# Prefix log-sum-exp on one core: three time steps per partition in place of two, Exp written over x, and later rows added to PSUM by VectorE

## The chip, the cores and the metric

The kernel runs on one NeuronCore of one Trainium2 chip. The metric is device time in microseconds (us), the median of several executions. Beside them stands one profiled execution, whose trace holds every instruction and every DMA packet with start and duration.

## What is computed

The input `x` has shape (4, 4096, 4128) in fp32: a batch of 4, 4096 time steps, 4128 features. The output is the running log-sum-exp along time:

```
out[:, 0, :] = x[:, 0, :]
for t in range(1, S):
    mx = max(out[:, t-1, :], x[:, t, :])
    out[:, t, :] = mx + log(exp(out[:, t-1, :] - mx) + exp(x[:, t, :] - mx))
```

That equals `log(cumsum(exp(x)))` along time, and so both kernels compute it: exponentials in fp16, a prefix sum by matmul in fp32 in PSUM, a logarithm, and a carry from tile to tile.

## The kernel before

One *tile* is a block of 256 consecutive time steps (`rows = P * R`, 128 partitions by `R = 2` rows, line 61) with all 4128 features. Partition p holds time steps 2p and 2p+1, one run of 33,024 bytes in device memory. There are 64 tiles, 16 for each batch, and each is loaded once and stored once (4128 KB each way).

The features of a tile are cut into four chunks of 1024 columns (`CH`); the last 32 columns, the *tail*, go with the fourth chunk. `Step.run` (lines 155 to 173) writes the order of all work out by hand under a manual schedule, so each engine takes its instructions in the order of the calls:

- `exp(c)` (line 107): ScalarE computes Exp of both rows of a chunk in one instruction, 128 x 2048 elements, into a separate fp16 tile `et` (pool of 4).
- `head(c)` (line 114): TensorE builds the prefix sum of row 0 in a PSUM tile `pt` of 128 x 1024 fp32 (two banks, pool of 3). Weights `incl` (partitions up to and with p) go with row 0, `excl` (partitions before p) with row 1, and `pick` fetches the carry of the tile before. That is six matmuls of 512 columns, four in the first tile of a batch.
- `ln(j, c)` (line 125): ScalarE writes Ln of the PSUM tile over row j of `xt`, in fp32.
- `second(c)` (line 128): TensorE adds row 1 to the same PSUM tile with two matmuls whose weights are the identity `ident`. `pt` then holds the prefix sum of row 1.
- `close(c)` (line 133): Ln of row 1, then `keep` (line 88): VectorE copies the last 32 partitions of `pt` to fp16 (line 90) and the rounding error beside it (line 91). This is the carry.
- `tail_mm` and `ln_tail` (lines 138, 148) do the same for the tail in a PSUM tile `qt`.

Loads and stores are all issued from SyncE's queue (SP). Five `xt` buffers exist (line 72). The load of tile i+3 is issued ahead of the work and the store of tile i (lines 176 to 184); it waits until the store of tile i-2 has landed, because both use one buffer.

Of the kernel before, what the change touches and what calls it, by code (L numbers as in the profile page):

```python
# [7 lines left out]
FP32 = mybir.dt.float32  # L8
FP16 = mybir.dt.float16
ACT = mybir.ActivationFunctionType  # L10
P = 128
R = 2
CH = 1024
MM = 512
HI, LO = 96, 32


def _constants(nc, pool):


    def tri(base, name):
        t = pool.tile([P, P], FP16, name=name)
        nc.gpsimd.memset(t, 1.0)

        nc.gpsimd.affine_select(  # L25
            out=t, in_=t, pattern=[[1, P]], compare_op=mybir.AluOpType.is_ge,
            fill=0.0, base=base, channel_multiplier=-1,
        )
        return t

    def ones_where_zero(bases, step, name):
        t = pool.tile([P, P], FP16, name=name)
        nc.gpsimd.memset(t, 0.0)
        for base in bases:
            nc.gpsimd.affine_select(  # L35
                out=t, in_=t, pattern=[[step, P]], compare_op=mybir.AluOpType.not_equal,
                fill=1.0, base=base, channel_multiplier=1,
            )
        return t

    return (
        tri(0, "incl"),
        tri(-1, "excl"),
        ones_where_zero([0], -1, "ident"),
        ones_where_zero([-(HI + 31), -(LO + 31)], 0, "pick"),
    )


@with_exitstack
def kernel(  # L50
    ctx: ExitStack,
    tc: tile.TileContext,
    x: bass.AP,
    out: bass.AP,
):

    nc = tc.nc
    B, S, D = x.shape  # L60
    rows = P * R
    n_t = S // rows
    assert S % rows == 0
    n_main = D // CH
    tail = D - n_main * CH
    t0 = n_main * CH

    nc.scalar.preload_act_table_set("natural_log_exp_and_others")  # L68
    consts = ctx.enter_context(tc.tile_pool(name="consts", bufs=1))
    incl, excl, ident, pick = _constants(nc, consts)  # L70

    xpool = ctx.enter_context(tc.tile_pool(name="xpool", bufs=5))
    epool = ctx.enter_context(tc.tile_pool(name="epool", bufs=4))
    cpool = ctx.enter_context(tc.tile_pool(name="cpool", bufs=1))
    pmain = ctx.enter_context(tc.tile_pool(name="pmain", bufs=3, space=bass.MemoryType.PSUM))
    ptail = ctx.enter_context(tc.tile_pool(name="ptail", bufs=2, space=bass.MemoryType.PSUM))

    carry = [cpool.tile([P, CH], FP16, name=f"carry{c}") for c in range(n_main)]
    carry_t = cpool.tile([P, tail], FP16, name="carry_t")
    for t in (*carry, carry_t):  # L80
        nc.vector.memset(t, 0.0)  # L81

    ctx.enter_context(tc.manual_schedule())

    def mm(pt, w, rhs, start, stop):
        nc.tensor.matmul(pt, lhsT=w, rhs=rhs, start=start, stop=stop, skip_group_check=True)  # L86

    def keep(cr, pt):

        nc.vector.tensor_copy(cr[HI:HI + 32, :], pt[HI:HI + 32])  # L90
        nc.vector.tensor_tensor(  # L91
            out=cr[LO:LO + 32, :], in0=pt[HI:HI + 32], in1=cr[HI:HI + 32, :],
            op=mybir.AluOpType.subtract,
        )

    class Step:
        def __init__(self, b, k):
            self.first = k == 0
            self.xt = xpool.tile([P, R, D], FP32, name="xt")
            self.et, self.pt = {}, {}  # L100
            self.dram = lambda t: t[b, k * rows:(k + 1) * rows, :].rearrange("(p j) d -> p j d", j=R)
            nc.sync.dma_start(out=self.xt, in_=self.dram(x))  # L102

        def cols(self, c):
            return slice(c * CH, (c + 1) * CH if c + 1 < n_main else D)

        def exp(self, c):
            s = self.cols(c)
            w = s.stop - s.start
            et = epool.tile([P, R, CH + tail], FP16, name="et")  # L110
            nc.scalar.activation(et[:, :, :w], self.xt[:, :, s], ACT.Exp)  # L111
            self.et[c] = et

        def head(self, c):
            et = self.et[c]
            pt = self.pt[c] = pmain.tile([P, CH], FP32, name="pt")
            for s in range(0, CH, MM):
                mm(pt[:, s:s + MM], incl, et[:, 0, s:s + MM], True, False)
            for s in range(0, CH, MM):
                mm(pt[:, s:s + MM], excl, et[:, 1, s:s + MM], False, self.first)  # L120
            if not self.first:
                for s in range(0, CH, MM):
                    mm(pt[:, s:s + MM], pick, carry[c][:, s:s + MM], False, True)

        def ln(self, j, c):
            nc.scalar.activation(self.xt[:, j, c * CH:(c + 1) * CH], self.pt[c], ACT.Ln)  # L126

        def second(self, c):
            pt = self.pt[c]
            for s in range(0, CH, MM):  # L130
                mm(pt[:, s:s + MM], ident, self.et[c][:, 1, s:s + MM], False, True)

        def close(self, c):

            self.ln(1, c)
            keep(carry[c], self.pt[c])

        def tail_mm(self):
            et = self.et[n_main - 1]
            qt = self.qt = ptail.tile([P, R, tail], FP32, name="qt")  # L140
            e0, e1 = et[:, 0, CH:], et[:, 1, CH:]
            for j in range(R):
                mm(qt[:, j, :], incl, e0, j == 0, False)
                mm(qt[:, j, :], incl if j else excl, e1, False, self.first)
                if not self.first:
                    mm(qt[:, j, :], pick, carry_t, False, True)

        def ln_tail(self):
            nc.scalar.activation(self.xt[:, :, t0:D], self.qt, ACT.Ln)  # L149
            keep(carry_t, self.qt[:, 1, :])  # L150

        def store(self):
            nc.sync.dma_start(out=self.dram(out), in_=self.xt)  # L153

        def run(self):
            last = n_main - 1
            self.exp(0)
            self.head(0)
            for c in range(1, n_main):
                self.exp(c)  # L160
                self.head(c)
                if c == last:
                    self.tail_mm()
                self.ln(0, c - 1)
                self.second(c - 1)
                if c >= 2:
                    self.close(c - 2)
            self.ln(0, last)
            self.second(last)
            self.close(last - 1)  # L170
            self.ln_tail()
            self.close(last)
            self.store()

    work = [(b, k) for b in range(B) for k in range(n_t)]
    ahead = 3
    steps = []
    for i, (b, k) in enumerate(work):
        if i == 0:
            steps += [Step(*work[n]) for n in range(ahead)]  # L180
        if i + ahead < len(work):
            n = i + ahead
            steps.append(Step(*work[n]))
        steps[i].run()


# [28 lines left out]
```

The softmax here doesn't subtract the row's maximum and nothing guards it: scores larger than these inputs give would overflow.

## Time and profile before

| | us |
|---|---|
| median of 10 runs (lowest, highest) | 1265.36 (1264.41, 1266.25) |
| the profiled execution, its own time | 1264.41 |
| its span, first to last instruction | 1262.6 |
| DMA queue of loads and stores, share of 16 engines' span | 99.5% |
| ScalarE busy | 962.6 (76%) |
| TensorE matmul busy | 665.4 (53%) |
| VectorE busy | 655.6 (52%) |

The span is what the instructions of the trace cover; the execution's own time is 1.8 us longer. 541.07 MB pass through the data queue, half in and half out, at a mean of 429 GB/s over the span. Busy shares are means over the span; they do not say which engine is waited for.

### The profile page before, as it was taken

The numbers are of one execution on the slowest core, as the hardware profiler recorded it, in microseconds if no ns is written. First come the engines' busy times: TensorE is split into PE (matmuls) and PEld (weight loads), VectorE is DVE, ScalarE is ACT, GpSimd is POOL, SyncE is SP. The second block draws the span as 40 slices with busy tenths as digits, with TensorE's granted clock in tenths as the row PEclk, the third lists the DMA queues.
The fourth block names the chain that finished last, engine by engine and source line by source line (L and its number), as shares of the span: only waits on it lengthen the run. The fifth ranks groups of instructions, "written<-read, shape, count | busy, mean of one in ns | idle before, by whom it ended". The sixth has DMA issues, their size and how long they took to land.

```text
span 1262.6 us, 7025 instructions
## 1 busy us (share of the span) xinstructions
PE 665.4 (53%) x2392; PEld 242.6 (19%) x2392; DVE 655.6 (52%) x645; ACT 962.6 (76%) x833; POOL 2.2 (0%) x13
## 2 busy tenths in 40 slices
PE   2566655545555465464554645546545555455551
PEld 1222221211112121121111212112112121121210
DVE  3556565464554544545545455464564544645543
ACT  6888887778777777786877878778778787787872
POOL 0000000000000000000000000000000000000000
PEclk9877788778687677867768777777767687777776
DMA  9999999999999999999999999999999999999997
GB/s 402 419 433 432 431 434 427 434 435 425 432 434 434 435 432 432 432 431 431 434 433 435 432 434 433 433 428 434 433 435 432 433 433 431 431 434 433 433 434 336
DMA packets 18466, 541.51 MB, mean 429 GB/s; under 512 B 2048, under 2 KB 2048, under 8 KB 2048
## 3 DMA queue, kind: packets, MB, share of 16 engines
q1 hardware_dynamic: 18432, 541.07, 99.5%
q8 instruction: 19, 0.31, 0.1%
q14 instruction: 15, 0.12, 0.0%
HBM read 270.53 MB, written 270.53 MB: 429 GB/s over the span
## 4 chain that ended last, share of the span: by engine, by line
DMA 84%; ACT 2%; SPq 1%; DVE 1%; issue 1%; PE 0%; ACTq 0%
DMA out_dram<-xt 80%; DMA xt<-in_x_dram 5%; ACT et L111 1%; ACT xt L126 1%; SPq L102 1%; PE pt L86 0%; DVE carry L90 0%; DVE carry L91 0%; SPq L153 0%; DVE carry_t L90 0%; DVE carry_t L91 0%; ACTq L126 0%
## 5 line engine op out<-in xcount | busy, mean ns | idle before, releaser
L90 DVE CAST carry<-pt 32x1024 f16<-32x1024 f32 x256 | 314.8, 1230 | 574.6 <-ACT xt L126 571.7
L126 ACT ACTIVATE xt<-pt 128x1024 f32<-128x1024 f32 x512 | 504.2, 1028 | 127.8 <-PE pt L86 67.1
L111 ACT ACTIVATE et<-xt 128x2048 f16<-128x2048 f32 (+1 forms) x256 | 485.5, 1921 | 148.8 <-DMA xt<-in_x_dram 148.8
L86 PE MATMUL pt<-et,incl 128*128 128x512 f16 x512 | 211.9, 507 | 547.6 <-ACT et L111 373.3
L91 DVE TENSOR_TENSOR carry<-pt,carry 32x1024 f16<-32x1024 f32 x256 | 313.9, 1226 | 8.8
L86 PE MATMUL pt<-et,excl 128*128 128x512 f16 x512 | 211.2, 505 | 0.0
L86 PEld LDWEIGHTS <-incl 128*128 128x128 f16 x704 | 69.2, 111 | 683.1 <-issue 635.5
L86 PE MATMUL pt<-carry,pick 128*128 128x512 f16 x480 | 195.1, 498 | 0.0
L86 PE MATMUL pt<-et,ident 128*128 128x512 f16 x512 | 175.5, 429 | 25.9 <-ACT xt L126 25.9
L86 PEld LDWEIGHTS <-excl 128*128 128x128 f16 x576 | 71.4, 124 | 117.4 <-issue 86.3
L86 PEld LDWEIGHTS <-pick 128*128 128x128 f16 x600 | 69.5, 118 | 94.5 <-issue 65.8
L86 PEld LDWEIGHTS <-ident 128*128 128x128 f16 x512 | 49.5, 106 | 100.5 <-issue 73.7
L86 PE MATMUL qt<-et,incl 128*128 128x32 f16 x192 | 19.9, 191 | 0.0
L86 PE MATMUL qt<-carry_t,pick 128*128 128x32 f16 x120 | 15.6, 182 | 0.0
L149 ACT ACTIVATE xt<-qt 128x64 f32<-128x64 f32 x64 | 14.6, 228 | 0.0
L90 DVE CAST carry_t<-qt 32x32 f16<-32x32 f32 x64 | 12.6, 196 | 2.0
L91 DVE TENSOR_TENSOR carry_t<-qt,carry_t 32x32 f16<-32x32 f32 x64 | 12.4, 193 | 2.2
L86 PE MATMUL qt<-et,excl 128*128 128x32 f16 x64 | 11.7, 183 | 0.0
L81 DVE MEMSET carry<- 128x512 uint32 x4 | 1.9, 485 | 1.1 <-PEq L199 1.0
L68 ACT ACT_TABLE_LOAD x1 | 1.3, 1283 | 0.8 <-PEq L199 0.8
L35 POOL TENSOR_SCALAR_AFFINE_SELECT pick<-pick 128x128 f16<-128x128 f16 x2 | 0.6, 292 | 0.1
L25 POOL TENSOR_SCALAR_AFFINE_SELECT incl<-incl 128x128 f16<-128x128 f16 x1 | 0.3, 292 | 0.0
(11 smaller groups left out, 1.9 us busy)
## 6 DMA issues: line engine op xcount, KB each, us to landing
xt<-in_x_dram SPq DMA_DIRECT2D x64, 4128.0 KB, 29.3
out_dram<-xt SPq DMA_DIRECT2D x64, 4128.0 KB, 38.6
```

Of the source, the lines that this page charges most:

```text
L25: nc.gpsimd.affine_select(out=t, in_=t, pattern=[[1, P]], compare_op=mybir.AluOpType.is_ge, fill=0.0, base=base, channel_multiplier=-1,)
L35: nc.gpsimd.affine_select(out=t, in_=t, pattern=[[step, P]], compare_op=mybir.AluOpType.not_equal, fill=1.0, base=base, channel_multiplier=1,)
L68: nc.scalar.preload_act_table_set("natural_log_exp_and_others")
L81: nc.vector.memset(t, 0.0)
L86: nc.tensor.matmul(pt, lhsT=w, rhs=rhs, start=start, stop=stop, skip_group_check=True)
L90: nc.vector.tensor_copy(cr[HI:HI + 32, :], pt[HI:HI + 32])
L91: nc.vector.tensor_tensor(out=cr[LO:LO + 32, :], in0=pt[HI:HI + 32], in1=cr[HI:HI + 32, :], op=mybir.AluOpType.subtract,)
L102: nc.sync.dma_start(out=self.xt, in_=self.dram(x))
L111: nc.scalar.activation(et[:, :, :w], self.xt[:, :, s], ACT.Exp)
L126: nc.scalar.activation(self.xt[:, j, c * CH:(c + 1) * CH], self.pt[c], ACT.Ln)
L149: nc.scalar.activation(self.xt[:, :, t0:D], self.qt, ACT.Ln)
```

## The change

`R` becomes 3. A tile holds 384 time steps, one run of 49,536 bytes for each partition. A batch has 32 blocks of 128 steps, so it is cut into ten tiles of three rows and one of two; in the first batch the small tile comes first, in the others last. That makes 40 tiles of three rows and 4 of two.

Exp of all three rows of a chunk is one instruction, and its fp16 result is written over the front half of the same fp32 columns of `xt` (`half` is `xt` seen as fp16). The pool `et` is gone, and `xt` has four buffers. The load of tile n+3 is issued after the store of tile n, on the same queue.

`second` and the weights `ident` are gone. After Ln of row j, VectorE adds row j+1 of the exponentials to the PSUM tile in place (`stage`, 128 x 1024, fp32 + fp16). `head` has two matmuls for each row and two for the carry, eight in a tile of three rows. The tail's rows are formed by matmuls with a broadcast right side.

Each tile runs a small pipeline over g: at each g, stage d of chunk g-d for d from high to low, then Exp of chunk g+2 and the head of chunk g+1. Exp of chunks 0 and 1 of the next tile comes after the last stage of this one. The diff, without the constants and the asserts:

```diff
-R = 2
+R = 3
...
-    def mm(pt, w, rhs, start, stop):
-        nc.tensor.matmul(pt, lhsT=w, rhs=rhs, start=start, stop=stop, skip_group_check=True)
+    def mm(pt, w, rhs, start=False):
+        nc.tensor.matmul(pt, lhsT=w, rhs=rhs, start=start, stop=False, skip_group_check=True)
...
-    xpool = ctx.enter_context(tc.tile_pool(name="xpool", bufs=5))
-    epool = ctx.enter_context(tc.tile_pool(name="epool", bufs=4))
+    bufs = 4
+    xpool = ctx.enter_context(tc.tile_pool(name="xpool", bufs=bufs))
...
+        def load(self):
+            full = xpool.tile([P, R, D], FP32, name="xt")
+            self.xt = full[:, :self.r, :]
+            self.half = self.xt.bitcast(FP16)
             nc.sync.dma_start(out=self.xt, in_=self.dram(x))
...
-        def second(self, c):
-            pt = self.pt[c]
-            for s in range(0, CH, MM):
-                mm(pt[:, s:s + MM], ident, self.et[c][:, 1, s:s + MM], False, True)
...
+        def e(self, j, a, b):
+            return self.t.half[:, j, 2 * self.c * CH + a:2 * self.c * CH + b]
+
+        def exp(self):
+            c0, w = self.c * CH, self.w
+            nc.scalar.activation(
+                self.t.half[:, :, 2 * c0:2 * c0 + w], self.t.xt[:, :, c0:c0 + w], ACT.Exp,
+            )
+
+        def head(self):
+            t = self.t
+            pt = self.pt = pmain.tile([P, CH], FP32, name="pt")
+            for j in range(t.r):
+                for s in range(0, CH, MM):
+                    mm(pt[:, s:s + MM], excl if j else incl, self.e(j, s, s + MM), start=j == 0)
+            if not t.first:
+                for s in range(0, CH, MM):
+                    mm(pt[:, s:s + MM], pick, carry[self.c][:, s:s + MM])
+            if self.c == last:
+                self.tail_head()
+
+        def tail_head(self):
+            t, r = self.t, self.t.r
+            full = ptail.tile([P, R, tail], FP32, name="qt")
+            qt = self.qt = full[:, :r, :]
+            to = lambda v, n: v.unsqueeze(1).to_broadcast([P, n, tail])
+            for i in range(r):
+                e = self.e(i, CH, CH + tail)
+                mm(qt[:, i:, :], incl, to(e, r - i), start=i == 0)
+                if i:
+                    mm(qt[:, :i, :], excl, to(e, i))
+            if not t.first:
+                mm(qt, pick, to(carry_t, r))
+
+        def stage(self, j):
+            t, c, pt = self.t, self.c, self.pt
+            nc.scalar.activation(t.xt[:, j, c * CH:(c + 1) * CH], pt, ACT.Ln)
+            if j + 1 < t.r:
+                nc.vector.tensor_tensor(
+                    out=pt, in0=pt, in1=self.e(j + 1, 0, CH), op=mybir.AluOpType.add,
+                )
+                if c == last and j == 0:
+                    nc.scalar.activation(t.xt[:, :, t0:D], self.qt, ACT.Ln)
+                    keep(carry_t, self.qt[:, t.r - 1, :])
+            else:
+                keep(carry[c], pt)
...
+    ahead = bufs - 1
+    for s in steps[:ahead]:
+        s.load()
+    for n, s in enumerate(steps):
+        chunks = [Chunk(s, c) for c in range(n_main)]
+        chunks[0].exp()
+        chunks[1].exp()
+        chunks[0].head()
+        for g in range(n_main + s.r - 1):
+            for d in range(s.r - 1, -1, -1):
+                if 0 <= g - d < n_main:
+                    chunks[g - d].stage(d)
+            if g + 2 < n_main:
+                chunks[g + 2].exp()
+            if g + 1 < n_main:
+                chunks[g + 1].head()
+        s.store()
+        if n + ahead < len(steps):
+            steps[n + ahead].load()
```

## Prediction

> **What bounds the kernel now.** I read the totals and the DMA rows first, then the list of waits, the groups, and last the timeline of one tile.
>
> ```profile
> PE 665.4 (53%) x2392; PEld 242.6 (19%) x2392; DVE 655.6 (52%) x645; ACT 962.6 (76%) x833; POOL 2.2 (0%) x13
> ...
> DMA  9999999999999999999999999999999999999997
> ...
> q1 hardware_dynamic: 18432, 541.07, 99.5%
> ```
> ```profile
> SPq L102 <- DMA out_dram<-xt: 1079.6, 59, 20.4
> ```
> ```profile
> DVE carry L90 <- ACT xt L126: 571.7, 161, 18.7
> ...
> ACT et L111 <- DMA xt<-in_x_dram: 148.8, 55, 11.1
> ```
>
> The data queue is busy for 99.5% of the span in every slice, the loads wait for stores (1079.6 us), ScalarE waits for loads (148.8 us). So the transfers set the end. In the trace a 33,024-byte packet follows another on its engine every 1.219 us, so 16 engines move 433.5 GB/s, and one tile (8.45 MB in and out) takes 19.5 us. The compute of a tile takes, in the last one, from the start of Exp of chunk 0 (1222.40) to the end of the last Ln (1239.95) 17.5 us. The margin is 2 us a tile, and it is what the change spends.
>
> The durations that I use:
>
> ```profile
> L90 DVE CAST carry<-pt 32x1024 f16<-32x1024 f32 x256 | 314.8, 1230 | 574.6 <-ACT xt L126 571.7
> L126 ACT ACTIVATE xt<-pt 128x1024 f32<-128x1024 f32 x512 | 504.2, 1028 | 127.8 <-PE pt L86 67.1
> ...
> L91 DVE TENSOR_TENSOR carry<-pt,carry 32x1024 f16<-32x1024 f32 x256 | 313.9, 1226 | 8.8
> ...
> L86 PE MATMUL pt<-et,ident 128*128 128x512 f16 x512 | 175.5, 429 | 25.9 <-ACT xt L126 25.9
> ```
> ```profile
> L111 ACT ACTIVATE et<-xt 128x2048 f16<-128x2048 f32 x192 | 359.2, 1904 | 148.8 <-DMA xt<-in_x_dram 148.8
> ```
> ```profile
> 1222.40 3.71 ACT L111 ACTIVATE et<-xt 128x2048 f16<-128x2048 f32 x2 [1.80 <-DMA xt<-in_x_dram]
> ...
> 1224.36 1.01 PE L86 MATMUL pt<-et,incl 128*128 128x512 f16 x2 [5.07 <-ACT et L111]
> 1225.17 1.06 PE L86 MATMUL pt<-et,excl 128*128 128x512 f16 x2
> 1226.03 1.06 PE L86 MATMUL pt<-carry,pick 128*128 128x512 f16 x2
> ...
> 1227.17 1.02 ACT L126 ACTIVATE xt<-pt 128x1024 f32<-128x1024 f32 x1 [1.06 <-issue]
> ...
> 1238.95 1.23 DVE L90 CAST carry<-pt 32x1024 f16<-32x1024 f32 x1 [0.94 <-ACT xt L126]
> 1240.22 1.23 DVE L91 TENSOR_TENSOR carry<-pt,carry 32x1024 f16<-32x1024 f32 x1
> 1241.47 0.20 DVE L90 CAST carry_t<-qt 32x32 f16<-32x32 f32 x1
> ```
>
> In the timeline a head of six matmuls takes 2.86 us from the end of the first Exp (1224.31) to Ln (1227.17), pairs following each other by 0.85 us. Two `keep` instructions take 2.52 us (1238.95 to 1241.47).
>
> **What the Trainium skill says.** "VectorE: DVE Perf Modes", section "The perf-mode tier table": tensor_tensor with a PSUM operand runs at one element a cycle. The page's (N+151)/0.96 gives 1.224 us for 1024; line 91 agrees (1.226). "ScalarE: Activation LUTs", section "What ACT_TABLE_LOAD costs": back-to-back ACTIVATEs overlap by about 93 ns; agrees (two Exps, 2 x 1.904 - 3.71 = 0.10). "TensorE: Matmul & The Clock Gate", Part 1: after an idle window of 3.4 us the array runs at half rate, 427 ns for 512 columns. The trace agrees: in 54 places the matmuls start after over 3.4 us without one, and of the first eight at least 87% follow at 0.427.
>
> **The change part by part.** *Transfers.* The bytes are the same. A three-row tile is 12.68 MB both ways, 29.25 us at 433.5 GB/s. Packets for each engine fall from 1024 to 704. At 27.2 B/ns (the 435 GB/s ceiling of "DMA: Bandwidth & Descriptors", Specifications; 433.5 here) a packet would take 1.214 us, so about 5 ns are fixed: 320 x 5 ns = 1.6 us gained at most. Runs of 193.5 x 256 B could give half of that back. *Queue.* On SP a load is now behind the store of tile n, which waits for the tile's last Ln. The load has two more tiles of compute before it is needed, 64 us against some 32 us for a store and a load: no cost; if that cover went, the start of a tile would wait for the load. Four buffers for five: covered likewise. *Exp in place:* same elements, no more work. *Identity matmuls gone:* 175.5 us of TensorE, beside other work; nothing on the path. *VectorE adds:* 40 x 8 + 4 x 4 = 336 of them, a new link between two Lns of the same chunk. No row shows 128 x 1024 from PSUM to PSUM. From below 1.07 us (1024 elements at the page's 0.96 GHz, nothing fixed), from above 1.39 (line 91's 0.16 us over that, counted once more for a write to PSUM); a conflict of read and write is rival B. A gain from the add itself is excluded: it only lengthens the way from Ln to Ln. I take line 91, 1.226, and 1.26 with the start of the next.
>
> *The chain of one three-row tile*, c chunk, r row. In the built order Exp of the next tile comes behind the last Ln of this, and the tail's Ln waits for the add of chunk 3 ahead of it; whatever stands behind it on ScalarE waits too.
>
> 1. Exp c0: 1.904 + (1.904 - 1.028) = 2.78.
> 2. Head of eight cold matmuls until Ln: 2.86 + 2 x 0.427 = 3.71. Exp c1 (2.78) lies beneath.
> 3. ScalarE until Ln of c0 r2 has ended: Ln c0 r0 (0.92 to the next), Exp c2 (2.81), Ln c0 r1 and c1 r0 (1.84), Exp c3 (2.89), Ln (1.02): 9.48.
> 4. VectorE without a gap: keep c0, two adds, keep c1, two adds: 2 x 2.52 + 4 x 1.26 = 10.05. Its Lns are done sooner. The head of c3, which needs the PSUM buffer of c0, is beneath.
> 5. Tail Ln (0.14 to the next), Ln c2 r2 (1.02): 1.16.
> 6. keep c2, then the last add: 2.52 + 1.23 = 3.75.
> 7. Ln c3 r2, until the next Exp: 0.92.
>
> With five handovers of 0.03 (ScalarE to VectorE in the trace): 32.0 us. That is over the 29.25 of the transfers, so the bound moves to the ScalarE-VectorE chain. DMA will wait 9% of the time.
>
> A two-row tile: 1.90 + 2.86 + 0.92 + 1.93 + 1.02, then three times (keep 2.52 + add 1.23 + two handovers 0.06), two Lns between (2.04) and 1.07 at the end = 23.2. The first of a batch has no `pick`: 0.85 less.
>
> Sum: first load landed 13.2 (Exp starts at 13.16 now, same size); first tile 22.3; 37 x 32.0 = 1184; 3 x 31.15 = 93.5; two small tiles 46.4; the last 23.3; its store 12.3 (the first load, issue at 0.80 to landing at 13.1); end 0.3. Together 1395 us of span. The execution's own time was 1.8 over its span, and the median 0.95 over that: 1398.
>
> **The rivals.** *A, the transfers stay the bound: not slower.* The point is a tile chain under 29.25 us. Five adds lie on the chain, so an add of at most 1.226 - 2.75/5 = 0.68 us decides, that is two elements a cycle. For it: fp16 on one input. Against: line 91 has the same kinds of inputs and takes 1.226. Time: 1265.4 - 1.6 + up to 0.8, about 1264. Chance 0.05. *B, the add reads and writes one PSUM bank at half rate:* 2.29 us, 1.07 more, 5 x 40 + 3 x 4 times: +227, 1625. For it: no such row in the trace. Against: nothing there shows a read slowed by other PSUM work. 0.07. *C, the head is not on the path,* because TensorE stays at full rate: Ln then starts when Exp c1 has ended, 0.93 sooner in 43 tiles: 1358. Against: between the head of c3 and the next tile TensorE has some 12 us without work. 0.06. *D, 49.5 KB runs transfer over 9% slower,* with DMA at 99%: 1400 or more; nothing in the profile speaks for it. 0.03.
>
> **How the numbers follow.** The main case has 0.79. Its own range: an add of 1.07 takes 0.156 x 212 = 33 us off, 1365; one of 1.39 adds 35; handovers from VectorE to ScalarE, not shown, of 0.15 as VectorE to TensorE takes (1234.89 to 1235.04 in the trace) in place of 0.03 add two times 0.12 in 44 tiles, 11; both at once would be 1444, which I think improbable, and I stop at 1435. The range 1358 to 1435 takes in C and leaves out A and B. Faster by over 0.2% 0.03, within 0.2% 0.02 (a difference that small couldn't be told from none in this kernel), slower 0.95.
>
> **What would show it.** The data queue's share falls to about 91%; SP's waits for a store to land give way to waits for ScalarE; VectorE busy near 860; Exp starts 32 us apart in three-row tiles; ScalarE has waits for VectorE, absent now, and for TensorE at the tile's start; the new add near 1.23 us. Wrong: a 99% data queue (A or D), an add under 0.7 or over 2, or a head at 216 ns for each matmul.

## The result, and the profile after

The changed kernel takes 1382.36 us (median of eight executions; 1381.89 to 1382.98), the kernel before 1265.36. The ratio is 1.0925, with a 95% interval from 1.0915 to 1.0934: 9% slower. The forecast was 1398, with a range from 1358 to 1435. The profiled execution has a span of 1380.1 us.

The totals of the changed kernel's page, in the order of those shown of before:

```profile
PE 481.5 (35%) x1596; PEld 181.2 (13%) x1596; DVE 853.4 (62%) x781; ACT 973.8 (71%) x733; POOL 1.8 (0%) x11
...
DMA  9999999999999999998999999999899999999847
...
q1 hardware_dynamic: 12672, 541.07, 93.2%
```

The same bytes now leave the data queue idle for 6.8% of a longer span. ScalarE is not busier than before (973.8 against 962.6 us); VectorE has 198 us more. No engine is near its limit. A page with no busy engine and a transfer queue that is not full suggests that engines wait for each other in turn. The chain of work that ended last, in shares of the span, is no longer that of transfers:

```profile
DVE 42%; ACT 42%; PE 10%; issue 4%; DMA 1%; ACTq 0%
```

The waits name the partners. First SP's own, then who waited for whom:

```profile
SPq L114 <- ACT xt L160: 1316.9, 44, 31.3
```
```profile
DVE pt L162 <- ACT xt L160: 312.4, 84, 14.9
...
ACT xt L160 <- DVE pt L162: 211.8, 88, 2.9
DVE carry L90 <- ACT xt L160: 174.1, 136, 2.3
ACT xt L166 <- DVE pt L162: 117.7, 44, 3.2
...
ACT xt L126 <- DMA xt<-in_x_dram: 11.0, 1, 11.0
```

Before, SP's long wait was that of a load for a store to land (1079.6 us). Now all 44 stores wait for a Ln (line 160), 1316.9 us in total, and ScalarE's 148.8 us of waiting for loads have shrunk to 11.0, the first load. ScalarE waits for VectorE (211.8 and 117.7 us), which it never did before, and VectorE for ScalarE (312.4 and 174.1 us). The two take turns. The groups confirm the price of the new instruction:

```profile
L162 DVE TENSOR_TENSOR pt<-pt,xt 128x1024 f32<-128x1024 f32 x336 | 402.0, 1229 | 316.5 <-ACT xt L160 312.4
```

One three-row tile in the timeline of the changed kernel, from its first Exp to that of the next tile (which has two rows); lines of other engines are left out, and so are some of ScalarE and VectorE where the dots stand:

```profile
635.38 5.55 ACT L126 ACTIVATE xt<-xt 128x3072 f16<-128x3072 f32 x2
...
641.79 1.02 ACT L160 ACTIVATE xt<-pt 128x1024 f32<-128x1024 f32 x1 [0.86 <-PE pt L86]
...
650.20 2.85 ACT L160 ACTIVATE xt<-pt 128x1024 f32<-128x1024 f32 x3
651.25 1.23 DVE L90 CAST carry<-pt 32x1024 f16<-32x1024 f32 x1 [2.34 <-ACT xt L160]
...
658.69 2.37 DVE L162 TENSOR_TENSOR pt<-pt,xt 128x1024 f32<-128x1024 f32 x2
661.15 0.25 ACT L166 ACTIVATE xt<-qt 128x96 f32<-128x96 f32 x1 [2.55 <-DVE pt L162]
661.30 1.94 ACT L160 ACTIVATE xt<-pt 128x1024 f32<-128x1024 f32 x2
...
662.35 1.23 DVE L90 CAST carry<-pt 32x1024 f16<-32x1024 f32 x1 [0.49 <-ACT xt L160]
...
664.87 1.23 DVE L162 TENSOR_TENSOR pt<-pt,xt 128x1024 f32<-128x1024 f32 x1
666.13 1.02 ACT L160 ACTIVATE xt<-pt 128x1024 f32<-128x1024 f32 x1 [2.90 <-DVE pt L162]
667.05 3.84 ACT L126 ACTIVATE xt<-xt 128x2048 f16<-128x2048 f32 x2
```

The brackets hold the idle time ahead of an instruction and who ended it. ScalarE stands still for 0.86 us at the head, for 2.55 us ahead of the tail's Ln and for 2.90 us ahead of the last Ln. From Exp to Exp it is 667.05 - 635.38 = 31.67 us; the median over the kernel is 31.68. The transfers of such a tile need 29.25 by the prediction's estimate, and the runs without adds and with one order over all tiles, below, come to it.

### The profile page after: what moved, and what is told of

Same layout as the page of the kernel before. It is cut to its first block, busy times and chain, and to the rows that moved or that the text cites. A ratio compares the mean times of both kernels' runs of the same rounds, so it can differ in the third digit from the quotient of the medians.

```text
span 1380.1 us, 5327 instructions
## 1 busy us (share of the span) xinstructions
PE 481.5 (35%) x1596; PEld 181.2 (13%) x1596; DVE 853.4 (62%) x781; ACT 973.8 (71%) x733; POOL 1.8 (0%) x11
## 3 DMA queue, kind: packets, MB, share of 16 engines
q1 hardware_dynamic: 12672, 541.07, 93.2%
## 4 chain that ended last, share of the span: by engine, by line
DVE 42%; ACT 42%; PE 10%; issue 4%; DMA 1%; ACTq 0%
ACT xt L126 25%; DVE pt L162 18%; ACT xt L160 16%; DVE carry L90 12%; DVE carry L91 12%; PE pt L86 10%; DMA xt<-in_x_dram 1%; ACT xt L166 1%; ACTq L227 0%; ACTq L166 0%; ACTq L160 0%
## 5 line engine op out<-in xcount | busy, mean ns | idle before, releaser
L160 ACT ACTIVATE xt<-pt 128x1024 f32<-128x1024 f32 x512 | 504.8, 1023 | 263.4 <-DVE pt L162 211.8
L162 DVE TENSOR_TENSOR pt<-pt,xt 128x1024 f32<-128x1024 f32 x336 | 402.0, 1229 | 316.5 <-ACT xt L160 312.4
L126 ACT ACTIVATE xt<-xt 128x3072 f16<-128x3072 f32 (+3 forms) x176 | 475.4, 2701 | 12.4 <-DMA xt<-in_x_dram 11.0
L86 PE MATMUL pt<-xt,incl 128*128 128x512 f16 x352 | 153.8, 532 | 876.6 <-ACT xt L126 615.5
L90 DVE CAST carry<-pt 32x1024 f16<-32x1024 f32 x176 | 216.4, 1229 | 175.3 <-ACT xt L160 174.1
L86 PE MATMUL pt<-xt,excl 128*128 128x512 f16 x672 | 258.7, 523 | 0.0
L91 DVE TENSOR_TENSOR carry<-pt,carry 32x1024 f16<-32x1024 f32 x176 | 215.9, 1226 | 6.1
L86 PEld LDWEIGHTS <-incl 128*128 128x128 f16 x480 | 53.0, 117 | 964.6 <-issue 927.8
L86 PE MATMUL pt<-carry,pick 128*128 128x512 f16 x320 | 127.9, 491 | 0.0
L86 PEld LDWEIGHTS <-excl 128*128 128x128 f16 x756 | 95.0, 127 | 147.2 <-issue 118.2
L166 ACT ACTIVATE xt<-qt 128x96 f32<-128x96 f32 (+1 forms) x44 | 10.9, 248 | 117.7 <-DVE pt L162 117.7
L86 PEld LDWEIGHTS <-pick 128*128 128x128 f16 x360 | 43.6, 121 | 65.1 <-issue 47.6
```

The costliest lines, as they stand in the source:

```text
L86: nc.tensor.matmul(pt, lhsT=w, rhs=rhs, start=start, stop=False, skip_group_check=True)
L91: nc.vector.tensor_tensor(out=cr[LO:LO + 32, :], in0=pt[HI:HI + 32], in1=cr[HI:HI + 32, :], op=mybir.AluOpType.subtract,)
L126: nc.scalar.activation(self.t.half[:, :, 2 * c0:2 * c0 + w], self.t.xt[:, :, c0:c0 + w], ACT.Exp,)
L160: nc.scalar.activation(t.xt[:, j, c * CH:(c + 1) * CH], pt, ACT.Ln)
L162: nc.vector.tensor_tensor(out=pt, in0=pt, in1=self.e(j + 1, 0, CH), op=mybir.AluOpType.add,)
L166: nc.scalar.activation(t.xt[:, :, t0:D], self.qt, ACT.Ln)
```

## The experiments

My theory was that the ScalarE-VectorE chain through one tile, which no other tile overlaps, sets the pace. Its main rivals: the transfers themselves (runs of 49.5 KB, four buffers, the load behind the store), too much work on VectorE, and TensorE. All medians stand beside 1265.0 to 1265.4 us of the kernel before on the same chips. "Pitch" is the median distance between first Exps of neighbouring tiles, counted in the trace; for kernels with tiles of three and of two rows it is that of the tiles of three.

**No add.**

```diff
-                nc.vector.tensor_tensor(
-                    out=pt, in0=pt, in1=self.e(j + 1, 0, CH), op=mybir.AluOpType.add,
-                )
```

> The changed kernel without the VectorE adds: rows 1 and 2 of a partition get the Ln of the same PSUM tile, so the later rows' terms are left out of the sum; all loads, stores, Exps, Lns and carries stay. If the chain from Ln to add to Ln sets the pace (my theory), it falls to the transfers: Exp starts of three-row tiles 29.2 us apart, data queue at 99%, about 1260 us. If runs of 49.5 KB, four buffers or the load behind the store are the cause, it stays within 1% of 1382 us.

Measured: 1262.56 us, ratio to before 0.9977 (0.9969 to 0.9986), pitch 29.25. Its page has

```profile
q1 hardware_dynamic: 12672, 541.07, 99.5%
```

So runs of 49.5 KB, four buffers and the order of SP's queue carry the transfers at their full rate. The rival of slow transfers is out, and so is the in-place Exp. In this order of work nothing is lost without the add. That doesn't yet say that the add alone is to blame: the order is tried further down.

**The adds given back to TensorE.**

```diff
-                nc.vector.tensor_tensor(
-                    out=pt, in0=pt, in1=self.e(j + 1, 0, CH), op=mybir.AluOpType.add,
-                )
+                for s in range(0, CH, MM):
+                    mm(pt[:, s:s + MM], ident, self.e(j + 1, s, s + MM))
```

(The weights `ident` are built as in the kernel before.)

> The changed kernel with its adds given back to TensorE as pairs of matmuls with identity weights; order, buffers, runs and tiles stay. Theory: VectorE has only the carries left, so the seven-step chain breaks up; a pair costs 0.85 us cold and about 0.3 to Ln, near the add's 1.23, but stands in another queue than the carries. I expect 1260 (the transfers) to 1300 us (if the head behind the pairs is late). If the in-place Exp, the buffers or the length of runs is the cause: 1382 us.

Measured: 1263.40 us, ratio 0.9984 (0.9978 to 0.9991), data queue 99.5%. This is complete work, far faster than the changed kernel and 0.16% under the kernel before. The sum of a row and its Ln still take turns, but with an engine that has no carries in its queue. TensorE's clock isn't the reason: the matmuls at the start of each tile stand 0.427 us apart here too.

**The tail's Ln one stage later.**

```diff
-                if c == last and j == 0:
+                if c == last and j == t.r - 2:
```

> One line: in a three-row tile the tail's Ln and carry move from row 0 to row 1 of the last chunk. Theory: the tail's Ln no longer holds up Ln of c2 row 2 behind the add of chunk 3, so the carry of c2 starts when that add ends and not 1.2 us later; 40 tiles x 1.1 us: about 1338 us, pitch 30.55. If ScalarE's place in the order is not on the path (VectorE or transfers alone set it): 1382 us.

Measured: 1341.52 us, ratio 1.0601 (1.0585 to 1.0617), pitch 30.62. A Ln of 0.25 us, moved together with its two small carries (0.20 and 0.19 us), is worth 41 us, because what stood behind it in ScalarE's queue (Ln of c2 row 2) is what the carry of c2 waits for. In the timeline of this kernel that carry begins with no wait for ScalarE, right behind the two adds, where the changed kernel had 0.49 us of idle time after two small carries:

```profile
639.37 2.36 DVE L162 TENSOR_TENSOR pt<-pt,xt 128x1024 f32<-128x1024 f32 x2
640.64 1.02 ACT L160 ACTIVATE xt<-pt 128x1024 f32<-128x1024 f32 x1 [1.52 <-DVE pt L162]
641.77 1.23 DVE L90 CAST carry<-pt 32x1024 f16<-32x1024 f32 x1
```

**One order over the chunks of all tiles.**

```diff
-    for n, s in enumerate(steps):
-        chunks = [Chunk(s, c) for c in range(n_main)]
-        chunks[0].exp()
...
+    chunks = [Chunk(s, c) for s in steps for c in range(n_main)]
+    chunks[0].exp()
+    chunks[1].exp()
+    chunks[0].head()
+    done = 0
+    for g in range(len(chunks) + R - 1):
+        for d in range(R - 1, -1, -1):
+            if 0 <= g - d < len(chunks) and d < chunks[g - d].t.r:
+                chunks[g - d].stage(d)
+        if g + 2 < len(chunks):
+            chunks[g + 2].exp()
+        if g + 1 < len(chunks):
+            chunks[g + 1].head()
...
```

(The store and the next load of a tile follow its last stage.)

> The same instructions with one order over the chunks of all tiles: Exp and head of the next tile come before the last stages of this one. Theory: the chain is the latency of a tile, not the throughput of an engine (ScalarE 22.5 us, VectorE 20 us of work in a three-row tile against 29.2 us of transfers), so overlapping tiles gives the transfers back the bound: 1258 to 1270 us. If VectorE or ScalarE is simply overloaded: about 1380 us.

Measured: 1276.18 us, ratio 1.0086 (1.0069 to 1.0103), pitch 29.25. Its page has

```profile
PE 554.5 (44%) x1596; PEld 181.9 (14%) x1596; DVE 849.3 (67%) x781; ACT 950.4 (75%) x733; POOL 1.8 (0%) x11
...
q1 hardware_dynamic: 12672, 541.07, 98.8%
```

The pace is that of the transfers again, with every add still on VectorE, which is busy for 849.3 of 1274.3 us. So VectorE isn't overloaded; the changed kernel suffers from the latency of a tile. But the time is outside what I expected, by 6 us.

**The same with the tail's Ln one stage later**, to find those microseconds; its edit is that of the tail above.

> The one order over all tiles, and the tail's Ln one stage later. With the stream alone the data queue was empty only near the start (2.4 us) and for some 8 us near the end; if these come from the same wait of ScalarE for the add, 1264 to 1270 us. If they come from the Exp of the next tile, which waits for its load with the last Lns of this tile behind it, the time stays near 1276 us.

Measured: 1275.54 us, ratio 1.0083 (1.0068 to 1.0098), no difference. The tail isn't it. The trace shows the place: no packet is under way for 2.5 us near the start (67 us), and between 1238 and 1246 us the queue runs dry (for its last 3.3 us without any packet). A tile in one stream has its stages spread between those of its neighbours: from its first Exp to its store it is 47 us (median of the tiles), against 32 in the changed kernel. As long as loads are left, they fill the queue; after the last one nothing does until the last stores come. That this is the whole of the gap was read from the trace and not tried by itself.

**TensorE kept at full rate.**

```diff
-    ptail = ctx.enter_context(tc.tile_pool(name="ptail", bufs=2, space=bass.MemoryType.PSUM))
+    ptail = ctx.enter_context(tc.tile_pool(name="ptail", bufs=1, space=bass.MemoryType.PSUM))
...
+    pwarm = ctx.enter_context(tc.tile_pool(name="pwarm", bufs=1, space=bass.MemoryType.PSUM))
+    warm = pwarm.tile([P, MM], FP32, name="warm")
...
+            if g + 1 == last:
+                for _ in range(40):
+                    mm(warm, incl, carry[0][:, :MM], start=True)
```

> The changed kernel with 40 extra matmuls of 512 columns behind the head of chunk 3 in each tile, into a spare PSUM bank, read by nobody (one tail buffer in place of two makes room). They fill most of the some 11 us in which TensorE has no work. Theory: the head of the next tile then runs at full rate, ends before Exp of chunk 1 has ended, and the first Ln starts 0.83 us sooner (5.58 in place of 6.41 after the tile's start): 43 x 0.83 = 36 us, about 1347. If TensorE isn't on the path: 1382. If the extra matmuls get in the way of the head: over 1382.

Measured: 1348.78 us, ratio 1.0662 (1.0646 to 1.0678), pitch 30.70. Forty matmuls in each tile whose results nobody reads make the kernel 34 us faster, though the tail has one buffer fewer. In its timeline the head takes pairs 0.43 us apart and Ln follows Exp without a wait:

```profile
618.90 5.55 ACT L129 ACTIVATE xt<-xt 128x3072 f16<-128x3072 f32 x2
...
621.71 0.59 PE L89 MATMUL pt<-xt,incl 128*128 128x512 f16 x2 [3.39 <-ACT xt L129]
622.14 1.02 PE L89 MATMUL pt<-xt,excl 128*128 128x512 f16 x4
...
624.36 1.00 ACT L163 ACTIVATE xt<-pt 128x1024 f32<-128x1024 f32 x1
```

Ln starts 5.46 us after the tile's start, and 6.41 us in the changed kernel (635.38 to 641.79). The second term of my chain was thus on the path, and its price was that of a half-rate TensorE. In 6 of the 43 tiles after the first the head's matmuls still stand 0.427 us apart in this run.

**Adds of half the columns.**

```diff
-                    out=pt, in0=pt, in1=self.e(j + 1, 0, CH), op=mybir.AluOpType.add,
+                    out=pt[:, :MM], in0=pt[:, :MM], in1=self.e(j + 1, 0, MM), op=mybir.AluOpType.add,
```

> The adds are done on 512 of 1024 columns only, so the later rows' terms are left out in half of the columns of each chunk. An add then takes about 0.70 us. The prediction put the point at which the transfers take over at 0.68 us. Theory: the chain shortens by 5 x 0.53 = 2.65 us to 29.0, as good as the 29.2 of the transfers: 1263 to 1275 us. If the cost of an add were its fixed part or the handover and not its length, the time would stay above 1320.

Measured: 1288.26 us, ratio 1.0186 (1.0169 to 1.0203), pitch 29.47: a miss of 13 us beyond the upper end. An add takes 0.70 us as expected, yet the chain gets 2.2 us shorter and not 2.65. The timeline shows where the difference goes:

```profile
611.02 1.30 DVE L162 TENSOR_TENSOR pt<-pt,xt 128x512 f32<-128x512 f32 x2
611.75 1.94 ACT L160 ACTIVATE xt<-pt 128x1024 f32<-128x1024 f32 x2 [1.46 <-DVE pt L162]
612.81 1.23 DVE L90 CAST carry<-pt 32x1024 f16<-32x1024 f32 x1 [0.49 <-ACT xt L160]
```

With short adds VectorE is done before ScalarE is, and the carry of c1 waits 0.49 us for a Ln: another path has become the longer one. And a chain at 29.5 us is not yet a kernel bound by transfers: its first tile (landed at 13 us) and its last tile and store (22 and 12) stay uncovered, and 13 + 21 + 37 x 29.47 + 3 x 28.6 + 2 x 21.7 + 22 + 12 is 1288.

**Two rows.**

```diff
-R = 3
+R = 2
```

> The changed kernel with R = 2 in place of 3, all else the same (64 tiles of 33 KB runs). If the long runs cost the time, it gets faster than 1382. Theory: it gets slower, since each tile pays its unhidden chain of 23.2 us for two rows and not 31.7 for three: 13 + 4 x 22.4 + 59 x 23.2 + 23 + 12 = 1507, with what lies around the span about 1510 us.

Measured: 1513.02 us (two runs), ratio 1.1962 (1.1938 to 1.1985), pitch 23.25, data queue 86.9%. The third row in itself helps this order, since a tile's unhidden chain is paid 44 times (40 of 31.68 us for three rows, four near 23.2) and not 64 times 23.25.

**One Exp ahead of the last stage.**

```diff
-        chunks = [Chunk(s, c) for c in range(n_main)]
-        chunks[0].exp()
+        chunks = tiles[n]
         chunks[1].exp()
...
+            if g == n_main + s.r - 2 and n + 1 < len(steps):
+                tiles[n + 1][0].exp()
             for d in range(s.r - 1, -1, -1):
```

> The changed kernel with one Exp moved: chunk 0 of the next tile is done ahead of the last stage (Ln of chunk 3, row 2) and not behind it. Theory: ScalarE stands idle there for 2.9 us, waiting for the carry of c2 and the last add; an Exp of 2.76 us fits in, so the chain is 31.68 - 2.76 = 28.9 us, under the 29.25 of the transfers. Then the transfers set the pace, the data queue is at 99% and, unlike with the one order over all tiles, only one Ln stands behind an Exp that waits for its load, so no gap at the end: 1262 to 1268 us. If VectorE's work itself is the limit, 1382.

Measured: 1265.20 us, ratio 0.9997 (0.9989 to 1.0005). The 117 us are gone with one Exp in another place, the adds as they were. The loads wait for stores again, and the queue is full:

```profile
SPq L111 <- DMA out_dram<-xt: 284.0, 33, 10.8
```
```profile
q1 hardware_dynamic: 12672, 541.07, 99.4%
```

In the timeline the Exp fills the hole ahead of the last Ln, and in this tile it waits for its load, as in a kernel bound by transfers (20 times in the run, the first load among them):

```profile
540.93 1.23 DVE L91 TENSOR_TENSOR carry<-pt,carry 32x1024 f16<-32x1024 f32 x1
541.99 2.76 ACT L126 ACTIVATE xt<-xt 128x3072 f16<-128x3072 f32 x1 [1.44 <-DMA xt<-in_x_dram]
542.19 1.23 DVE L162 TENSOR_TENSOR pt<-pt,xt 128x1024 f32<-128x1024 f32 x1
544.65 1.01 ACT L160 ACTIVATE xt<-pt 128x1024 f32<-128x1024 f32 x1
```

Where it doesn't wait, the pitch is 27.9 us: 3.8 less than 31.7, more than the 2.76 of the Exp that I had counted on. The next tile's head now begins while the last Ln runs, and the first Ln's wait for it (0.86 us a tile in the changed kernel) is gone from this run's list of waits.

**Two rows in one order over all tiles**, with six buffers, the carries of a step issued behind its adds.

```diff
-R = 3
+R = 2
...
-    bufs = 4
+    bufs = 6
...
-            else:
-                keep(carry[c], pt)
...
+        for d in range(R - 1, -1, -1):
+            if 0 <= g - d < len(chunks) and d == chunks[g - d].t.r - 1:
+                keep(carry[chunks[g - d].c], chunks[g - d].pt)
```

> Tiles of two rows (runs of 33 KB, six buffers) with VectorE adds and Exp in place, one order over all tiles, the carries of a step behind its adds, the tail's Ln as in the changed kernel for two rows. Theory: neither the adds nor the two rows cost anything by themselves once tiles overlap: the transfers set the end, 1262 to 1272 us against 1513 for two rows in the order of the changed kernel. Packets of 33 KB in place of 49.5 KB cost 1.6 us against the Exp-moved kernel if both are bound by transfers to the end.

Measured: 1265.44 us, ratio 1.0001 (0.9993 to 1.0009), pitch 19.50, that of the kernel before. The same two rows and the same adds that took 1513 us take 1265 when tiles overlap. Two more buffers and the place of the carries changed with the order, so what each of the three is worth is not shown. The 1.6 us that I expected between runs of 33 and 49.5 KB can't be seen against the kernel with one Exp moved: 1265.44 against 1265.20, with ranges that overlap.

## Why the prediction was right

**The bound moved.** Right: the chain of a tile passed 29.25 us, and the transfers come back when the adds are left out (1262.56), go to another engine (1263.40), or stay and one Exp of the next tile overlaps them (1265.20).

**The chain, step by step**, predicted and read from the timeline above:

| step | predicted | measured |
|---|---|---|
| 1 Exp c0 | 2.78 | 2.76 |
| 2 head until Ln | 3.71 | 3.66 |
| 3 ScalarE until Ln c0 r2 has ended (651.22) | 9.48 | 9.43 |
| 4 VectorE, two carries and four adds (651.25 to 661.06) | 10.05 | 9.81 |
| 5 tail Ln and Ln c2 r2 (661.15 to 662.32) | 1.16 | 1.17 |
| 6 carry of c2 and the last add (662.35 to 666.10) | 3.75 | 3.75 |
| 7 last Ln until the next Exp | 0.92 | 0.92 |
| handovers | 0.15 | 0.18 |
| sum | 32.0 | 31.68 |

**Where the 15 us of span went.** The prediction's span was 1395, the measured 1380.1. The largest term is step 4: I let each add start 0.03 us after the one ahead of it, as the carries do. In the trace an add behind an add starts 0.09 us before that one ends (120 cases), and two take 2.37 us in place of 2.52. With the smaller differences that is 0.32 us in each of 40 tiles of three rows, 13 us; tiles that ran under the median, some at 31.3, make about 2 more. The price of one add was right: 1.229 us measured, 1.226 taken from line 91.

**The smaller forecasts.** The data queue has 93.2% where about 91% was forecast, VectorE 853.4 us (near 860). The waits of ScalarE for VectorE and for TensorE at the tile's start came as forecast. Three readings of the profile before were loose, and none enters the sum: the queue is full in every slice but the last, which stands at 7; the handover of 0.15 us from VectorE to TensorE lies at 1234.34 to 1234.49, not at 1234.89; and behind the 54 pauses of TensorE the first two matmuls start 0.38 us apart and the next five spacings are 0.427 in at least 51 places.

**The rivals.** A (an add of at most 0.68 us leaves the transfers as the bound) had the right mechanism, but its point was reckoned wrongly. With the measured chain of 31.68, five adds of 0.70 in place of 1.23 us would give 29.0, under 29.25; measured were 29.47, and 1288 us. I had counted all five adds as on the path whatever their length; the trace of that run shows a Ln taking over. Where the transfers do take over was not measured. B (half rate in PSUM) is out by the 1229 ns. C (the head not on the path) was priced at 40 us and brought 34: 1348.78 with a busy TensorE, from 1382.36, and some heads stayed slow. D (slow long runs) is out by the run without adds. The two tiles of cover for the loads held: no tile after the first waited for its load.

**What stays open.** The run without adds is 0.2% faster than the kernel before. Fewer packets (704 for each DMA engine in place of 1024, priced at up to 1.6 us) and fewer instructions to fetch (4907 in place of 7025) are both candidates. Two runs with nearly the same number of instructions speak for the packets: the adds on TensorE (6165 instructions, 704 packets) take 1263.40, and two rows in one order (6123 instructions, 1024 packets) 1265.44, with intervals of the ratio that don't touch. But they differ in their order too, and the run with one Exp moved has 704 packets and takes 1265.20. No run moved the carries of the changed kernel alone, though three of them, 2.5 us each, lie on its chain. The up to 0.8 us for runs of 193.5 x 256 bytes wasn't tried by itself.

## What to carry to other kernels

When a transfer-bound kernel has a small margin for each tile, ask for the latency of a tile from its first instruction to the first of the next, not for the busy share of an engine: here no engine passed 71%, and 9% were lost. An operation that is moved to another engine brings its own place in that engine's queue; put between two steps of the same data and behind unrelated work (here the carries), its length and that of its neighbours can lie on the path. Look for the holes in the engine that the chain comes back to, and put an instruction of the next tile there before changing the arithmetic.

## What the runs showed of the hardware

- An add of 128 x 1024 from PSUM to PSUM with one fp16 operand takes 1.229 us, and the subtraction of 32 x 1024 from PSUM to SBUF 1.226; writing PSUM in place costs 0.003 us more.
- Two adds in a row without idle time overlap by 0.09 us (120 cases), while a carry right behind an add starts 0.03 us after its end (40 cases). The Trainium skill, "VectorE: DVE Perf Modes", section "Two Vector instructions with no wait between them", gives a model: an instruction is held until all earlier ones have finished if an input or its output starts in another quadrant (a group of 32 partitions) than the last one read from or written to the same memory. Adds start at partition 0 and carries at 96, so the trace agrees, and I had not used it.
- TensorE with 12 us of idle time in each tile runs each head at half rate: pairs of matmuls stand 0.85 us apart, and 0.43 in most tiles once 40 unread matmuls fill the hole. That took 34 us off a kernel in which TensorE is busy for 35% of the time.
- Packets of 49,536 bytes take 1.829 us (median) and packets of 33,024 bytes 1.222, the same for each byte within 0.3%.
